# A streaming-encoder block: the embedding's loads and splits in a new order, and the gate's product and residual by whole rows

## The chip, the cores and the metric

The kernel runs on one core of one Trainium2 chip. The metric is device time in microseconds (us) of one execution; lower is better. The inputs and the output are float32 in DRAM; most matrix products are made from two fp32r parts of each operand, a high part and the remainder ("hi" and "lo"), with three matmuls (hi·hi, hi·lo, lo·hi).

## The reference, cut to what matters

```python
h = _layer_norm(x, ln_in_g, ln_in_b)
proj = h @ w_in[i]
...
mix = jnp.concatenate([o_gdn, o_fox], axis=-1) @ w_out[i]
h = _layer_norm(ALPHA * h + mix, ln1_g[i], ln1_b[i])
ff = jnp.square(jax.nn.relu(h @ w_up[i])) @ w_down[i]
ple = (p[i] @ w_ple[i]) * jax.nn.sigmoid(h @ w_ple_gate[i] + b_ple_gate[i])
h = _layer_norm(ALPHA * h + ff + ple, ln2_g[i], ln2_b[i])
```

There are 1024 tokens of width 1024; the embedding p has 256 columns, the expansion 4096.

## The kernel before, in words

The program is one long straight line of instructions. A tile scheduler orders them on each engine by program order, by priorities and by its own idea of when data are there; each engine then works through its queue strictly in that order, and semaphores hold an instruction until its inputs are there. SP issues nearly all DMAs, also in order. ACT and DVE share the splitting of operands: ACT casts the high part, DVE subtracts it from the source for the low part.

**The start.** SP loads the embedding p in two halves (`p_raw`, L227 and L239), w_ple in two halves of 512 columns (`w_raw_ple`, L233 in `load_ple`), rows of x (`load_x`), and the columns of w_in for the values in eight pieces (`wvr`, `load_wv`, L249). `load_ple` also casts and subtracts at once (L234, L54). `ple_prep(half)` transposes half of p on PE (`ps_pT`, L266), casts it on ACT (`pT_hi`, L268) and subtracts on DVE (`pT_lo`, L269). `ple_mm(t, n)` makes one block of p @ w_ple, 128 tokens by 512 columns, in six matmuls (`ps_ple`, L278), scales it by 0.5 on ACT (`ple_o`, L279) and stores it to `ple_spill` (L280). The matmuls rotate through three PSUM banks. Then come the LayerNorm of x, its transposes (`ps_tr`, L156) and the value projection (`psv`, L309), and from there the projections, the two attention groups and the output mix.

**The gate.** h @ w_ple_gate is a Strassen-like scheme of seven products for each of two halves of 256 columns (`prod`, `ps_gP`, L1075). `vals` and `plus` collect the products with the bias in a tile `gv` of 512 rows by 256 columns. `gout` takes tanh on ACT; then for each half of the rows it loads the embedding `pl` and the residual `hb`, makes (gv + 1)·pl and hb·ALPHA + gv on DVE (both at L51, the helper `stt`) and stores to `acc_spill`. It is called eight times. The same stage prepares tokens 4 to 7's blocks with `rest(j)`: three loads (`r`, L1122 to L1124, the last from `t_spill`), two DVE subtractions, transposes.

**The expansion.** `mlp_up(c)`, sixteen times, makes seven products of 12 matmuls (`ps_uP`, L1208), with operand splits `uA` and `uS` on ACT and DVE through a ring of five tiles, and the sums and activations on DVE. The last stage multiplies by w_down and adds `acc_spill`, which `with_acc` loads (L1350).

What sets the order around the change: SP's, ACT's and DVE's queues as the scheduler fills them; `tc.issue_after(x)` makes the scheduler place a step behind x; `tc.high_priority` and `tc.cur_priority` shift steps. `slot(...)` names the pool tile that a step reuses: `ph` and `pl` hold one tile of 512 KB each, `cv` and `th` three of 256 KB each.

Of the kernel before, what the change touches and what calls it, by code (L numbers as in the profile page):

```python
# [8 lines left out]
F32 = mybir.dt.float32  # L9
# [17 lines left out]
ALPHA = 2.0 ** 0.25  # L27
# [5 lines left out]
def _sl(i, n=P):  # L33
    return slice(i * n, (i + 1) * n)
# [3 lines left out]
def tile_block(ctx: ExitStack, tc: tile.TileContext, x, p, ln_in_g, ln_in_b, w_in, conv_w, a_log, dt_bias,  # L38
               gdn_norm_g, b_f, fox_norm_g, w_out, ln1_g, ln1_b, w_up, w_down, w_ple, w_ple_gate,
               b_ple_gate, ln2_g, ln2_b, out):  # L40
    nc = tc.nc
    PS = bass.MemoryType.PSUM
    x, p, out = x[0], p[0, 0], out[0]
# [6 lines left out]
    def stt(o, a, s, b, op0, op1):  # L50
        nc.vector.scalar_tensor_tensor(out=o, in0=a, scalar=s, in1=b, op0=op0, op1=op1)  # L51

    def split_lo(eng, lo, src, hi):
        eng.tensor_tensor(out=lo, in0=src, in1=hi.bitcast(F32), op=ALU.subtract)  # L54
# [157 lines left out]
    with tc.tile_pool(name="start", bufs=2, reuse_waits="tile") as stp:  # L212
# [16 lines left out]
        def load_ple(n):  # L229

            w = [wpool.tile([P, 2, 512], dt, tag=tag, name=f"{tag}_ple{n}")
                 for tag, dt in (("w_raw", F32), ("w_hi", F32R), ("w_lo", F32R))]
            nc.sync.dma_start(out=w[0], in_=w_ple[:, _sl(n, 512)].rearrange("(k q) c -> q k c", q=P))  # L233
            nc.scalar.copy(out=w[1], in_=w[0])  # L234
            split_lo(nc.vector, w[2], w[0], w[1])
            return w[1:]

        wpl = [load_ple(0)]
        nc.sync.dma_start(out=pt[:, 4:8], in_=pv[:, 4:8])  # L239
        load_x(0)  # L240
        wpl.append(load_ple(1))
        nc.gpsimd.dma_start(out=gb, in_=ln_in_g.partition_broadcast(P))
        nc.gpsimd.dma_start(out=bb, in_=ln_in_b.partition_broadcast(P))
        wvs = stp.tile([P, NK, 8], F32, name="wv_s", bufs=1)
# [17 lines left out]
        def ple_prep(half):  # L262
            for k in range(2):
                ps = sm("ps_pT")
                for i in range(4):
                    nc.tensor.transpose(ps[:, _sl(i)], pt[:, half * 4 + i, _sl(k)], ident)  # L266
                hi = pth[:, k, _sl(half, 512)]
                nc.scalar.copy(out=hi, in_=ps)  # L268
                lo = nc.vector.tensor_tensor(out=ptl[:, k, _sl(half, 512)], in0=ps, in1=hi.bitcast(F32), op=ALU.subtract)  # L269
            return lo.ins  # L270

        def ple_mm(t, n):
            so = stp.tile([P, 512], F32, tag="po", name="ple_o", bufs=5)
            ps = pj("ps_ple")
            wh, wl = wpl[n]
            for k in range(2):
                for wi, (aa, w) in enumerate(((pth, wh), (pth, wl), (ptl, wh))):
                    nc.tensor.matmul(ps, aa[:, k, _sl(t)], w[:, k], start=(k == 0 and wi == 0), stop=(k == 1 and wi == 2))  # L278
            nc.scalar.mul(out=so, in_=ps, mul=0.5)  # L279
            nc.sync.dma_start(out=ple_rows[t, :, _sl(n, 512)], in_=so)  # L280

        prep0 = ple_prep(0)
        with tc.issue_after(prep0):
            nc.vector.tensor_copy(out=wv_hi[:, :, 520:528], in_=wvs)
            split_lo(nc.vector, wv_lo[:, :, 520:528], wvs, wv_hi[:, :, 520:528])
        for t in range(4):
            ple_mm(t, 0)
        ple_prep(1)
        for t in range(4):
            ple_mm(t, 1)  # L290
# [5 lines left out]
        for t in range(NT):  # L296
# [8 lines left out]
            for n in range(2):  # L305
                ps = pj(f"psv{t}")
# [796 lines left out]

    def gout(v, n, h, t0):

        cs = slice(n * 512 + h * 256, n * 512 + h * 256 + 256)
        nc.scalar.activation(out=v, in_=v, func=AF.Tanh, scale=0.5)
        for jj in range(2):
            rows = slice(t0 * 512 + jj * 256, t0 * 512 + jj * 256 + 256)
            pl, hb = (cp.tile([P, 2, 256], F32, tag=tag, name=name, bufs=3) for tag, name in (("cv", "pl"), ("th", "hb")))  # L1110
            nc.sync.dma_start(out=pl, in_=ple_spill[rows, cs].rearrange("(j q) c -> q j c", q=P))
            nc.sync.dma_start(out=hb, in_=h1_spill[rows, cs].rearrange("(j q) c -> q j c", q=P))
            vj = v[:, 2 * jj:2 * jj + 2]
            stt(vj, vj, 1.0, pl, ALU.add, ALU.mult)
            stt(vj, hb, ALPHA, vj, ALU.mult, ALU.add)
            nc.sync.dma_start(out=acc_spill[rows, cs].rearrange("(j q) c -> q j c", q=P), in_=vj)

    def rest(j):

# [69 lines left out]
    def mlp_up(c):  # L1189
        raw = uraw.pop(c)  # L1190
        a = {f"A{f + 1}{k + 1}": raw[f][:, 4 * k:4 * k + 4] for f in range(2) for k in range(2)}
        s31, s24 = slot("kl1", [P, 2, 4, P], "wS31"), slot("va", [P, 2, 4, P], "wS24")
        a.update({"S3": s31[:, 0], "S1": s31[:, 1], "S2": s24[:, 0], "S4": s24[:, 1]})
        ua, ub = (slot(key, [P, 2, 512], name) for key, name in (("hi", "ua"), ("lo", "ub")))
        da, db = (slot("va", [P, 2, 512], name) for name in ("da", "db"))
        ps = {}

        def prod(p, chain=None):
            s, t = PAIR[p]
            v = slot(HL[hl[0] % 5], [P, 2, 4, P], f"u{s}", F32R)  # L1200
            hl[0] += 1
            hi, lo = v[:, 0], v[:, 1]
            nc.scalar.copy(out=hi, in_=a[s])  # L1203
            split_lo(nc.vector, lo, a[s], hi)
            ps[p] = ps[chain] if chain else (pj if p == "P2" else sm)(f"ps_u{p}")
            for k in range(4):
                for wi, (w, b) in enumerate(((hi, 0), (hi, 1), (lo, 0))):
                    nc.tensor.matmul(ps[p], w[:, k], B[t][b][k], start=(chain is None and k == 0 and wi == 0),  # L1208
                                     stop=(k == 3 and wi == 2), skip_group_check=chain is not None)
            return ps[p]  # L1210

        def keep(v, p):
# [24 lines left out]
        for nm in ("A11", "A12", "A22", "S3", "S1", "S2", "S4"):
            nc.sync.dma_start(out=r_spill[nm, c // 4][c % 4], in_=d[nm])
# [234 lines left out]
```

## Time and profile before

| | |
|---|---|
| runs | 1410.28, 1412.11, 1414.26 us (median 1412.11) |
| the profiled execution | 1411.87 us, span 1410.1 us |
| PE busy | 1375.8 us, 98% of the span, 7342 matmuls |
| PE weight loads busy | 1165.8 us, 83% |
| DVE busy | 1084.5 us, 77% |
| ACT busy | 559.3 us, 40% |
| DMA | 232.74 MB, mean 165 GB/s |
| mean granted clock of PE | 0.996 |

An engine is busy while it executes; a matmul's end is modelled, and matmuls overlap, so a row's duration is longer than the distance to the next. A wait is put down to the semaphore that came last. "Issue" of a DMA is when SP's instruction starts, "landing" when its semaphore rises.

### The profile page before, as it was taken

The page shows a single profiled execution, that of the slowest core. Times are in us where ns is not written, and L with a number is a line of the kernel's source. Part 1 is how long each engine was busy: PE and PEld are TensorE (multiplying, and loading weights), DVE is VectorE, ACT ScalarE, POOL GpSimd, SP SyncE. Part 2 cuts the span into 40 slices and gives each one's busy share as a digit, 9 for nine tenths or more (in the row PEclk, how much of TensorE's full clock was granted, in tenths as well). Part 3 has the DMA queues.
Part 4 walks back from the last instruction along what each step waited for, and adds up shares of the span by engine and source line. Part 5 has one row for each costly group of instructions (what it writes and reads, how often), then busy time and mean ns, then how long its engine had stood idle before and what let it go on. Part 6 is the DMA issues. An engine that isn't in the chain of part 4 may idle for free.

```text
span 1410.1 us, 20582 instructions
## 1 busy us (share of the span) xinstructions
PE 1375.8 (98%) x7342; PEld 1165.8 (83%) x7342; DVE 1084.5 (77%) x2273; ACT 559.3 (40%) x1044; POOL 15.4 (1%) x32
## 2 busy tenths in 40 slices
PE   7999999999999999999989999999999999999997
PEld 5997888988898887777889888888888888888885
DVE  6968899578566888968988766777666898748867
ACT  5323443243226767721133333333333444555421
POOL 1000000000000000000000000000000000000000
PEclk9999999999999999999999999999999999999999
DMA  9825434445478765234666744444446893334342
GB/s 304 282 104 180 150 83 116 146 157 149 127 190 199 172 150 166 68 133 168 214 215 207 237 137 153 157 160 147 148 131 228 315 342 111 97 97 125 117 134 83
DMA packets 193470, 232.74 MB, mean 165 GB/s; under 512 B 41638, under 2 KB 121687, under 8 KB 193367
## 3 DMA queue, kind: packets, MB, share of 16 engines
q1 hardware_dynamic: 187750, 226.69, 51.4%
q10 hardware_dynamic: 5232, 3.67, 1.0%
q8 instruction: 58, 0.95, 0.3%
q0 software_dynamic: 384, 1.06, 0.2%
q14 instruction: 46, 0.37, 0.1%
HBM read 155.29 MB, written 76.09 MB: 164 GB/s over the span
## 4 chain that ended last, share of the span: by engine, by line
PE 51%; DVE 3%; DMA 3%; issue 1%; SPq 0%; ACT 0%; DVEq 0%; ACTq 0%
PE ps_uP L1208 22%; PE ps_db L1328 9%; PE ps_da L1328 9%; PE ps_gP L1075 4%; PE ps_mix L954 3%; PE ps_db L1433 3%; DMA r<-t_spill 1%; DVE h L51 1%; PE ps_tr L961 1%; DMA h<-h_spill 0%; DMA wo_raw<-in_w_out_dram 0%; DMA hb<-h_spill 0%; DMA gA<-in_w_ple_gate_dram 0%; DMA h_spill<-h 0%; DVE gv L51 0%
## 5 line engine op out<-in xcount | busy, mean ns | idle before, releaser
L1208 PE MATMUL ps_uP<-T,uS 128*128 128x512 f32 x576 | 133.5, 390 | 0.0
L1208 PEld LDWEIGHTS ps_uP<-T,uS 128*128 128x128 f32 x576 | 108.1, 188 | 23.0
L1298 ACT CAST rh<-rr 128x512 fp32r<-128x512 f32 x112 | 69.9, 624 | 138.4 <-PE ps_db L1328 49.4
L54 DVE TENSOR_TENSOR rl<-rr,rh 128x512 fp32r<-128x512 f32 x112 | 77.1, 689 | 61.2 <-ACT rh L1298 22.3
L1208 PE MATMUL ps_uP<-B,uA 128*128 128x512 f32 x384 | 92.4, 396 | 0.0
L1208 PEld LDWEIGHTS ps_uP<-B,uA 128*128 128x128 f32 x384 | 72.2, 188 | 17.4
L954 PE MATMUL ps_mix<-wo,act_hi 128*128 128x512 f32 x256 | 81.7, 396 | 0.3 <-ACT act_hi L834 0.3
L207 PE MATMUL g<-act_hi,in_hi 128*128 128x512 f32 x192 | 75.5, 393 | 0.0
L207 PE MATMUL g<-act_hi,in_lo 128*128 128x512 f32 x192 | 75.3, 392 | 0.0
L207 PE MATMUL g<-act_lo,in_hi 128*128 128x512 f32 x192 | 74.9, 390 | 0.0
L54 DVE TENSOR_TENSOR uA<-uraw,uA 128x512 fp32r<-128x512 f32 x48 | 33.2, 691 | 47.8 <-ACT uA L1203 47.8
L1298 ACT CAST rl<-B 128x512 fp32r<-128x512 f32 x96 | 59.7, 623 | 24.5 <-PE ps_db L1328 11.5
L1203 ACT CAST uS<-wS 128x512 fp32r<-128x512 f32 x64 | 39.5, 624 | 73.0 <-issue 48.2
L54 DVE TENSOR_TENSOR ql<-B,rl 128x512 fp32r<-128x512 f32 x96 | 65.8, 686 | 0.3
L54 DVE TENSOR_TENSOR ptl<-ps_pt,pth 128x512 fp32r<-128x512 f32 (+2 forms) x96 | 51.1, 552 | 6.7 <-ACT pth L782 6.4
L954 PEld LDWEIGHTS ps_mix<-wo,act_hi 128*128 128x128 f32 x256 | 47.3, 188 | 10.1 <-DVE wo L54 0.6
L782 ACT CAST pth<-ps_pt 128x512 fp32r<-128x512 f32 (+2 forms) x96 | 44.4, 479 | 26.1 <-PE ps_pt L780 24.9
L51 DVE SCALAR_TENSOR_TENSOR cv<-g,hcw,cv 128x511 f32<-128x511 f32 (+2 forms) x72 | 52.8, 737 | 1.7 <-ACT cv L414 1.4
L764 ACT ACTIVATE s<-s,m 128x128 f32<-128x128 f32 (+3 forms) x64 | 49.9, 780 | 8.5 <-DVE m L761 7.8
L1328 PE MATMUL ps_db<-rl,rh 128*128 128x512 f32 x192 | 51.3, 389 | 0.0
L1328 PE MATMUL ps_db<-ql,rh 128*128 128x512 f32 x192 | 51.3, 389 | 0.0
L1328 PE MATMUL ps_db<-rl 128*128 128x512 f32 x192 | 51.3, 389 | 0.0
(358 smaller groups left out, 3586.0 us busy)
## 6 DMA issues: line engine op xcount, KB each, us to landing
uraw<-in_w_up_dram SPq DMA_DIRECT2D x32, 512.0 KB, 4.6
B<-in_w_down_dram SPq DMA_DIRECT2D x32, 512.0 KB, 5.1
rr<-rS SPq DMA_DIRECT2D x64, 256.0 KB, 2.6
in_raw<-in_w_in_dram SPq DMA_DIRECT2D x24, 512.0 KB, 4.3
rr<-rA SPq DMA_DIRECT2D x48, 256.0 KB, 2.8
h_spill<-h SPq DMA_DIRECT2D x16, 512.0 KB, 3.5
rA<-ub SPq DMA_DIRECT2D x32, 256.0 KB, 2.2
rS<-da SPq DMA_DIRECT2D x32, 256.0 KB, 2.1
```

Source lines behind the costliest of these rows:

```text
L51: nc.vector.scalar_tensor_tensor(out=o, in0=a, scalar=s, in1=b, op0=op0, op1=op1)
L54: eng.tensor_tensor(out=lo, in0=src, in1=hi.bitcast(F32), op=ALU.subtract)
L207: mm = nc.tensor.matmul(ps, w[:, k, :], a[n][:, :, k], start=(k == 0 and wi == 0), stop=(k == NK - 1 and wi == 2))
L764: nc.scalar.activation(out=s[:, :W], in_=s[:, :W], func=AF.Exp, bias=m[:, i:i + 1], scale=-1.0, accum_out=pairs[h // 2][2][:, r, j:j + 1])
L782: nc.scalar.copy(out=hi, in_=pt[:, :kn])
L954: nc.tensor.matmul(ps, a[t // 4][:, t % 4, k], w, start=(k == 0 and wi == 0), stop=(k == NK - 1 and wi == 2))
L1075: nc.tensor.matmul(ps[j // 2][:, j % 2], B[b][s][k][:, _sl(j)], a[w][:, k], start=(first and j % 2 == 0 and k == 0 and wi == 0), stop=(j % ...
L1203: nc.scalar.copy(out=hi, in_=a[s])
L1208: nc.tensor.matmul(ps[p], w[:, k], B[t][b][k], start=(chain is None and k == 0 and wi == 0), stop=(k == 3 and wi == 2), skip_group_check=c ...
L1298: nc.scalar.copy(out=hi, in_=src)
L1328: nc.tensor.matmul(ps[j], rs[x][:, _sl(j)], qs[y], start=(not chain and c == 0 and wi == 0), stop=(c == NP - 1 and wi == 2), skip_group_ch ...
L1433: nc.tensor.matmul(b[j], rs[x][:, i, _sl(j - js[0])], Q[c0 + i][y], start=(c0 == 0 and i == 0 and wi == 0), stop=(c0 + i == NP - 1 and wi ...
```

## The change

Two edits that don't touch each other.

The start: `load_ple` only loads. Both halves of w_ple are loaded directly behind the first half of p, ahead of its second half. The cast and subtraction are a step of their own, `split_ple(n)`; the first is placed behind the cast of the first half of p (`hi0`), the second behind the third scaled output block (`o[2]`).

The gate: `gout` ends with the tanh and one store of the tile, 512 KB. The product with the embedding and the residual move into `gated(t)`, which takes whole rows: for each block of 128 tokens it reads `acc_spill`, `h1_spill` and the two halves of `ple_spill`, makes the same two DVE operations for each half, and stores the rows back to `acc_spill`. It is called behind `mlp_up(c)` for c = 0 to 7. The 32 DVE operations are the same in number and size (128x512); 16 loads of `pl`, 16 of `hb` and 16 stores of 256 KB leave the gate, and 8 stores of 512 KB take their place; the expansion gets 16 loads of 512 KB, 16 of 256 KB and 8 stores of 512 KB.

```diff
             nc.sync.dma_start(out=w[0], in_=w_ple[:, _sl(n, 512)].rearrange("(k q) c -> q k c", q=P))
-            nc.scalar.copy(out=w[1], in_=w[0])
-            split_lo(nc.vector, w[2], w[0], w[1])
-            return w[1:]
-
-        wpl = [load_ple(0)]
+            return w
+
+        def split_ple(n):
+            nc.scalar.copy(out=wpl[n][1], in_=wpl[n][0])
+            split_lo(nc.vector, wpl[n][2], wpl[n][0], wpl[n][1])
+
+        wpl = [load_ple(n) for n in range(2)]
         nc.sync.dma_start(out=pt[:, 4:8], in_=pv[:, 4:8])
         load_x(0)
-        wpl.append(load_ple(1))
...
-        prep0 = ple_prep(0)
+        hi0, prep0 = ple_prep(0)
+        with tc.issue_after(hi0):
+            split_ple(0)
...
-        for t in range(4):
-            ple_mm(t, 0)
+        o = [ple_mm(t, 0) for t in range(4)]
+
+        with tc.issue_after(o[2]):
+            split_ple(1)
         ple_prep(1)
...
     def gout(v, n, h, t0):
...
         nc.scalar.activation(out=v, in_=v, func=AF.Tanh, scale=0.5)
-        for jj in range(2):
-            rows = slice(t0 * 512 + jj * 256, t0 * 512 + jj * 256 + 256)
-            pl, hb = (cp.tile([P, 2, 256], F32, tag=tag, name=name, bufs=3) for tag, name in (("cv", "pl"), ("th", "hb")))
-            nc.sync.dma_start(out=pl, in_=ple_spill[rows, cs].rearrange("(j q) c -> q j c", q=P))
-            nc.sync.dma_start(out=hb, in_=h1_spill[rows, cs].rearrange("(j q) c -> q j c", q=P))
-            vj = v[:, 2 * jj:2 * jj + 2]
-            stt(vj, vj, 1.0, pl, ALU.add, ALU.mult)
-            stt(vj, hb, ALPHA, vj, ALU.mult, ALU.add)
-            nc.sync.dma_start(out=acc_spill[rows, cs].rearrange("(j q) c -> q j c", q=P), in_=vj)
+        nc.sync.dma_start(out=acc_spill[_sl(t0, 512), n * 512 + h * 256:n * 512 + h * 256 + 256]
+                          .rearrange("(j q) c -> q j c", q=P), in_=v)
+
+    def gated(t):
+
+        v, hb = slot("ph", [P, 2, 512], "gt"), slot("pl", [P, 2, 512], "hb")
+        pl = [cp.tile([P, 512], F32, tag=tag, name="ple", bufs=3) for tag in ("cv", "th")]
+        nc.sync.dma_start(out=v.rearrange("q n c -> q (n c)"), in_=acc_spill[_sl(t), :])
+        nc.sync.dma_start(out=hb.rearrange("q n c -> q (n c)"), in_=h1_spill[_sl(t), :])
+        for n in range(2):
+            nc.sync.dma_start(out=pl[n], in_=ple_spill[_sl(t), _sl(n, 512)])
+        for n in range(2):
+            stt(v[:, n], v[:, n], 1.0, pl[n], ALU.add, ALU.mult)
+            stt(v[:, n], hb[:, n], ALPHA, v[:, n], ALU.mult, ALU.add)
+        nc.sync.dma_start(out=acc_spill[_sl(t), :], in_=v.rearrange("q n c -> q (n c)"))
...
         mlp_up(c)
+        if c < NT:
+            gated(c)
```

How the order of instructions moves, at three places.

ACT from its first cast on, before. `w_hi_ple` is the high part of half a w_ple, `pT_hi` of the transposed p, `wv_hi` of a piece `wvr` of w_in's value columns; `ple_o` is a scaled output block.

```order
L234 CAST w_hi_ple_130<-w_raw_ple_129 128x1024
L268 CAST pT_hi<-ps_pT 128x512 x2
L234 CAST w_hi_ple_139<-w_raw_ple_138 128x1024
L250 CAST wv_hi<-wvr_148 128x520
L279 ACTIVATE ple_o<-ps_ple 128x512
L250 CAST wv_hi<-wvr_152 128x520
L250 CAST wv_hi<-wvr_156 128x520
L279 ACTIVATE ple_o<-ps_ple 128x512
```

The same place on ACT in the change.

```order
L269 CAST pT_hi<-ps_pT 128x512 x2
L251 CAST wv_hi<-wvr_144 128x520
L237 CAST w_hi_ple_130<-w_raw_ple_129 128x1024
L251 CAST wv_hi<-wvr_148 128x520
L251 CAST wv_hi<-wvr_152 128x520
L251 CAST wv_hi<-wvr_156 128x520
L269 CAST pT_hi<-ps_pT 128x512 x2
L280 ACTIVATE ple_o<-ps_ple 128x512
L251 CAST wv_hi<-wvr_162 128x520
L280 ACTIVATE ple_o<-ps_ple 128x512 x2
L237 CAST w_hi_ple_134<-w_raw_ple_133 128x1024
L251 CAST wv_hi<-wvr_166 128x520
```

The first cast of w_ple went from the head of ACT's queue to behind the first piece of `wvr`; the second went from behind p's first half to behind the third output block, with three more `wvr` casts (166, 170, 174) between it and the next output block. DVE's subtractions stand in the same order: `w_lo_ple` behind `wv_lo` of the first piece, and the second behind those of 166, 170 and 174. On PE the transposes of p's second half, which stood behind the first 24 matmuls of `ps_ple`, now stand directly behind those of the first half:

```order
L267 MATMUL ps_pT<-ident,p_raw 128x128 x16
L279 MATMUL ps_ple<-w_hi_ple_130,pT_hi 128x512 x3
L279 MATMUL ps_ple<-w_lo_ple_131,pT_hi 128x512
L279 MATMUL ps_ple<-w_hi_ple_130,pT_lo 128x512
L279 MATMUL ps_ple<-w_hi_ple_130,pT_hi 128x512
```

The sixteen transposes are one run; the first three matmuls with the high part go to three banks before the first with the low part.

SP in the gate, around the loads of `rest(2)`, before: `r_7842` is the tile whose second half comes from `t_spill`, `uraw` the first columns of w_up.

```order
L1112 DMA hb<-h_spill 128x2x256
L1111 DMA pl<-ple_spill 128x2x256 x2
L1116 DMA acc_spill<-gv 128x2x256 x2
L1122 DMA r_7841<-h_spill 128x1024
L1123 DMA r_7842<-h_spill 128x512
L1124 DMA r_7842<-t_spill 128x512
L1122 DMA r_7871<-h_spill 128x1024
L1186 DMA uraw_0_8465<-in_w_up_dram 128x8x128
```

The same place in the change (here the tile is `r_7816`).

```order
L1123 DMA ple<-ple_spill 128x512 x4
L1113 DMA acc_spill<-gv 128x4x256
L1133 DMA r_7815<-h_spill 128x1024
L1134 DMA r_7816<-h_spill 128x512
L1197 DMA uraw_0_8361<-in_w_up_dram 128x8x128
L1135 DMA r_7816<-t_spill 128x512
L1133 DMA r_7845<-h_spill 128x1024
```

One store that needs only the tanh stands where two stores stood that need the DVE operations; the load of `uraw` now stands ahead of the load from `t_spill`.

DVE in the expansion, from one sum of a product to the next in c = 2 of the change. The row with `gt` and `ple` is `gated(2)`'s first operation; its other three stand a little later. Without it the rows are those of before, in nearly the same order.

```order
L48 TENSOR_TENSOR ua<-ua,ps_uP_8590 128x512
L54 TENSOR_TENSOR uS_8744<-wS_8683,uS_8744 128x512
L51 SCALAR_TENSOR_TENSOR ua<-ua 128x512
L51 SCALAR_TENSOR_TENSOR gt<-gt,ple 128x512
L48 TENSOR_TENSOR da<-ua 128x512
L48 TENSOR_TENSOR da<-ua,ub 128x512
L51 SCALAR_TENSOR_TENSOR ub<-ub 128x512
L48 TENSOR_TENSOR db<-ub,da 128x512
L48 TENSOR_TENSOR wS_8684<-uraw_1_8524,wS_8683 128x512
L48 TENSOR_TENSOR db<-ub,db 128x512
L48 TENSOR_TENSOR wS_8684<-uraw_0_8522,wS_8684 128x512
L54 TENSOR_TENSOR uS_8728<-wS_8684,uS_8728 128x512
```

One operation is added ahead of the split `uS_8728`, which the third product of the next c needs.

## Rows read from the trace of the kernel before

**Rows 1.** Windows: length, busy us of PE, PEld, DVE, ACT, POOL; PEclk, DMA share, GB/s.
```profile
5.50:37.30 31.80, 28.62 (x113) 21.86 (x114) 22.89 (x58) 17.99 (x30) 0.00 (x0) 1.00 0.96 333
37.30:690.00 652.70, 642.07 (x3801) 550.53 (x3800) 514.49 (x1295) 272.76 (x573) 11.33 (x18) 1.00 0.52 152
690.00:740.00 50.00, 44.08 (x359) 42.81 (x358) 45.52 (x71) 15.28 (x23) 0.00 (x0) 1.00 0.73 243
...
786.00:1095.00 309.00, 309.00 (x1348) 252.74 (x1347) 220.51 (x350) 102.37 (x179) 0.00 (x0) 1.00 0.51 166
```

**Rows 2.** Timeline of PE, 0 to 60: start, us, operation; [idle before, releaser].
```profile
5.49 1.94 PE L266 MATMUL ps_pT<-ident,p_raw 128*128 128x128 f32 x8 [5.49 <-DMA p_raw<-in_p_dram]
8.90 0.80 PE L278 MATMUL ps_ple<-w_hi_ple,pT_hi 128*128 128x512 f32 x1 [1.48 <-ACT pT_hi L268]
...
14.41 0.39 PE L278 MATMUL ps_ple<-w_hi_ple,pT_lo 128*128 128x512 f32 x1
14.64 0.39 PE L278 MATMUL ps_ple<-w_hi_ple,pT_hi 128*128 128x512 f32 x1
...
17.71 0.50 PE L278 MATMUL ps_ple<-w_hi_ple,pT_hi 128*128 128x512 f32 x1 [1.51 <-ACT ple_o L279]
...
37.28 1.25 PE L156 MATMUL ps_tr<-ident,h 128*128 128x128 f32 x10
```

**Rows 3.** Timeline of ACT, 0 to 45.
```profile
8.27 1.07 ACT L268 CAST pT_hi<-ps_pT 128x512 fp32r<-128x512 f32 x2
15.41 1.05 ACT L234 CAST w_hi_ple<-w_raw_ple 128x1024 fp32r<-128x1024 f32 x1 [6.07 <-DMA w_raw_ple<-in_w_ple_dram]
16.54 0.63 ACT L250 CAST wv_hi<-wvr 128x520 fp32r<-128x520 f32 x1
```

**Rows 4.** Timeline of SP, 0 to 45: the issue of the first four pieces.
```profile
4.04 8.84 SPq L249 DMA_DIRECT2D wvr<-in_w_in_dram  x4
```

**Rows 5.** DMA issues from 1.5 to 4.3: count, KB each, median us to landing.
```profile
p_raw<-in_p_dram SPq DMA_DIRECT2D x1, 512.0 KB, 7.8
...
wvr<-in_w_in_dram SPq DMA_DIRECT2D x1, 260.0 KB, 12.5
```

**Rows 6.** Timeline of DVE, 0 to 45.
```profile
16.57 1.21 DVE L54 TENSOR_TENSOR w_lo_ple<-w_raw_ple,w_hi_ple 128x1024 fp32r<-128x1024 f32 x1
17.69 2.76 DVE L54 TENSOR_TENSOR wv_lo<-wvr,wv_hi 128x520 fp32r<-128x520 f32 x4
```

**Rows 7.** Waits of PE, 40 to 60: us in total, times, longest.
```profile
PE psv L309 <- DVE act_lo L54: 0.9, 1, 0.9
```

**Rows 8.** Groups of DVE, shapes apart, 700 to 795: busy, mean ns; idle before.
```profile
L51 DVE SCALAR_TENSOR_TENSOR gv<-hb,gv 128x512 f32<-128x512 f32 x16 | 10.8, 689 | 1.2 <-DMA hb<-h_spill 1.1
...
L51 DVE SCALAR_TENSOR_TENSOR gv<-gv,pl 128x512 f32<-128x512 f32 x16 | 10.4, 687 | 2.3 <-ACT gv L1107 2.3
```

**Rows 9.** Timeline of PE, 728 to 746: the two waits.
```profile
730.75 0.66 PE L961 MATMUL ps_tr<-ident,r 128*128 128x128 f32 x4 [0.99 <-DVE T L54]
...
737.39 1.06 PE L961 MATMUL ps_tr<-ident,r 128*128 128x128 f32 x8 [1.79 <-issue]
```

**Rows 10.** Timeline of DVE, 684 to 790: the subtractions of `rest(2)`.
```profile
736.60 1.29 DVE L48 TENSOR_TENSOR r<-r,r 128x512 f32<-128x512 f32 x2 [1.50 <-DMA r<-t_spill]
```

**Rows 11.** Timeline of SP, 728 to 738: the load that they wait for.
```profile
731.45 0.44 SPq L1124 DMA_DIRECT2D r<-t_spill  x1
```

**Rows 12.** Timeline of DVE, 786 to 830: three splits and what follows.
```profile
809.05 1.89 DVE L54 TENSOR_TENSOR uS<-wS,uS 128x512 fp32r<-128x512 f32 x3
```

**Rows 13.** Timeline of PE, 784 to 830: products three to five of c = 1.
```profile
811.04 8.35 PE L1208 MATMUL ps_uP<-T,uS 128*128 128x512 f32 x36
```

**Rows 14.** DMA issues from 600 to 690: whole rows, 512 KB.
```profile
h<-h_spill SPq DMA_DIRECT2D x8, 512.0 KB, 4.0
...
h_spill<-h SPq DMA_DIRECT2D x7, 512.0 KB, 3.0
```

**Rows 15.** Windows: one stretch at the end of the attention.
```profile
574.20:577.60 3.40, 3.25 (x15) 3.11 (x16) 2.28 (x9) 1.99 (x6) 0.00 (x0) 0.50 0.53 169
```

More of the change, by code (lines that the diff above doesn't have):

```diff
@@ L267, in ple_prep @@
                 hi = pth[:, k, _sl(half, 512)]
-                nc.scalar.copy(out=hi, in_=ps)
+                last_hi = nc.scalar.copy(out=hi, in_=ps)
                 lo = nc.vector.tensor_tensor(out=ptl[:, k, _sl(half, 512)], in0=ps, in1=hi.bitcast(F32), op=ALU.subtract)
-            return lo.ins
+            return last_hi.ins, lo.ins
         def ple_mm(t, n):
@@ L274, in ple_mm @@
             ps = pj("ps_ple")
-            wh, wl = wpl[n]
+            wh, wl = wpl[n][1:]
             for k in range(2):
@@ L278, in ple_mm @@
                     nc.tensor.matmul(ps, aa[:, k, _sl(t)], w[:, k], start=(k == 0 and wi == 0), stop=(k == 1 and wi == 2))
-            nc.scalar.mul(out=so, in_=ps, mul=0.5)
+            o = nc.scalar.mul(out=so, in_=ps, mul=0.5)
             nc.sync.dma_start(out=ple_rows[t, :, _sl(n, 512)], in_=so)
-        prep0 = ple_prep(0)
+            return o.ins
+        hi0, prep0 = ple_prep(0)
+        with tc.issue_after(hi0):
+            split_ple(0)
         with tc.issue_after(prep0):
@@ L1104, in gout @@
     def gout(v, n, h, t0):
-        cs = slice(n * 512 + h * 256, n * 512 + h * 256 + 256)
         nc.scalar.activation(out=v, in_=v, func=AF.Tanh, scale=0.5)
-        for jj in range(2):
-            rows = slice(t0 * 512 + jj * 256, t0 * 512 + jj * 256 + 256)
-            pl, hb = (cp.tile([P, 2, 256], F32, tag=tag, name=name, bufs=3) for tag, name in (("cv", "pl"), ("th", "hb")))
-            nc.sync.dma_start(out=pl, in_=ple_spill[rows, cs].rearrange("(j q) c -> q j c", q=P))
-            nc.sync.dma_start(out=hb, in_=h1_spill[rows, cs].rearrange("(j q) c -> q j c", q=P))
-            vj = v[:, 2 * jj:2 * jj + 2]
-            stt(vj, vj, 1.0, pl, ALU.add, ALU.mult)
-            stt(vj, hb, ALPHA, vj, ALU.mult, ALU.add)
-            nc.sync.dma_start(out=acc_spill[rows, cs].rearrange("(j q) c -> q j c", q=P), in_=vj)
+        nc.sync.dma_start(out=acc_spill[_sl(t0, 512), n * 512 + h * 256:n * 512 + h * 256 + 256]
[11 more added lines that the diff above has]
+        nc.sync.dma_start(out=acc_spill[_sl(t), :], in_=v.rearrange("q n c -> q (n c)"))
     def rest(j):
```

## The prediction

> **What bounds the kernel now.** I read the windows first. From 37.3 us to 690 PE is busy 642.07 of 652.70 us, in the expansion 309.00 of 309.00 [rows 1]: the matmuls, which the change neither adds nor removes, set the time, and a change can win or lose only what PE waits or runs at a slow clock. There is 3.2 us of waiting in 5.5 to 37.3, 10.6 in 37.3 to 690, and 5.9 in the gate's first 50 us [rows 1]. So three places are to be costed: the start, the gate, and the expansion, which now waits for nothing and could begin to.
>
> The timelines of the start show how it hangs together. PE transposes p's first half at 5.49 as it lands, begins p @ w_ple at 8.90 and reaches the transposes of the LayerNorm at 37.28; from 14.41 to 14.64 two matmuls of 512 columns start 0.23 us apart [rows 2]. ACT casts p at 8.27, waits 6.07 us for the second w_ple, and casts the first piece of the value weights only at 16.54 [rows 3]; that piece was issued at 4.04 [rows 4] and landed 12.5 us later, at 16.5 [rows 5]. Three banks being full, PE waited 1.51 us up to 17.71 [rows 2], because the scaled output stood behind that second w_ple cast.
>
> **The start, term by term.** The change should let w_ple's cast follow p's. The instruction order says otherwise: on ACT the first w_ple cast now stands behind the cast of that first value piece. SP still issues two halves of p, two of w_ple, a block of x and a small piece ahead of it, the same bytes as before, so I take the same landing, 16.5. ACT then needs 0.6 for that cast (0.63 in [rows 3]) and 1.05 for w_ple [rows 3], and the first matmul goes from 8.90 to about 18.15: 9.25 later. That p's second half lands later costs nothing beyond this: it landed at about 9.5 as third transfer (7.8 after an issue at about 1.7, [rows 5]), the second w_ple at 15.4 as fifth [rows 3], so as fourth about 12.4, and its eight transposes end by 14.4 (1.94 in [rows 2]).
>
> From 18.15 on I count 96 matmuls. At 0.23 that is 22.2 us. Before, those from 8.90 to 14.41 ran at the low level of 1.2 GHz, some 13 of them at 0.42 instead of 0.23 (5.51 us for 13 starts, [rows 2]); I take the same 2.6 us of loss again. New waits: behind w_ple's first cast ACT has three value casts, two of p, then the outputs. The third bank fills at about 24.9, its output is out at 25.6, and the second w_ple cast, placed behind that, ends at 26.65; PE, done with its fourth block at 26.3, waits 0.35. After two matmuls it needs the fourth block's bank, whose output stands behind three value casts (1.6 us): until 28.8, a wait of 1.7. Then it needs the second low part, which DVE makes behind three subtractions of value pieces at 0.69 (2.76 for four, [rows 6]) in 1.2 [rows 6]: until 30.15, another 1.15. Sum 3.2. PE reaches the LayerNorm's transposes at 18.15 + 22.2 + 2.6 + 3.2 = 46.15, against 37.28: **+8.9**. Bounds: +6.0 if the piece lands a microsecond early and only 0.35 + 1 of the new waits come true, +10.5 if it lands a little late and the waits are a microsecond longer.
>
> What lies behind it? DVE finishes the first LayerNorm rows by about 39 (its work until then is shifted by at most 5 us) and is no longer late when PE comes; the wait of 0.9 for a low part [rows 7] should go: **−0.9**. The other waits up to 690 hang on results that PE itself gives, and move with it: 0.
>
> **The gate.** The 32 operations that leave are 16 at 0.689 and 16 at 0.687 us [rows 8], 21.2 us of DVE, and DVE's waits for `hb` of 1.1. But PE waits there only 5.9 in all [rows 1], and for particular things. The longest is 1.79 up to 737.39 [rows 9]: the transposes wait for `rest(2)`'s subtraction at 736.60, which itself waited 1.50 for its load from `t_spill` [rows 10], issued at 731.45 [rows 11], 5.1 before. SP was late with it because two stores of the gate stood ahead, waiting for the DVE operations that go. In the change the load of `uraw` stands ahead instead; it waits for a split on DVE, which about five operations fewer bring forward by some 2 us. I take issue at 729.7, landing at 734.8, one split ahead on DVE, the subtraction at 735.6 and the transposes at 736.25: 1.1 earlier, and four matmuls more done before (0.5). The wait of 0.99 at 730.75 for a split [rows 9] shortens on the way. Of the 1.6, 0.1 may be lost at `rest(3)`: **−1.5**. Bounds: 0, if `uraw`'s DVE wait takes the stores' place in full, and −3.0, half of the stage's 5.9. The tile `gv` is now stored whole by one DMA of 512 KB; its slot is needed again only several products later.
>
> **The expansion.** DVE is busy 220.5 of 309 us [rows 1]; the 21.2 come back in the first 155 us and make it 131 of 155. Enough on average, but DVE works in order. In c one operation (0.69) stands ahead of the split for the third product. Before, the first of three splits from 809.05 was done by 809.7 and its product began at 811.04 [rows 12, 13]: 1.35 us of slack, so 0.65 stays. That operation also waits for a row load that may start only when the previous rows' store has landed, in one slot. The stage frees DVE for `gated(c−1)`'s last operation about 4.7 us behind the start of that product (eight operations at 0.6, 1.89 for three in [rows 12]); 3.0 for the store and 4.0 for the load [rows 14] give 11.8, and the operation is due at 13.1 (19.3 a round, 84 matmuls at 0.23, less the 6.2 from there to the product). It holds by 1.3. In c = 0 the chain is tanh, store, load: about 3.0 + 0.4 + 3.5 + 4.0 = 11 behind the stage's start, and the sum that frees a bank follows by 15.3, due at 16.4. **0**, with bounds 0 and +3 (c = 0 a microsecond or two late, a little in each round). SP has idle time between issues here, and the stores `rA` and `rS` queued behind the waiting load have a round to land; the loads of `uraw` are a round ahead. If that cover is gone the price is the second rival. The extra 8.4 MB of traffic is 54 GB/s on the 166 of this stage [rows 1].
>
> **The sum.** 1411.87 + 8.9 − 0.9 − 1.5 + 0 = 1418.4 us. This stands against the profiled execution, 0.2 below the median of the runs; a difference of about 0.3%, 4.2 us, is what can be told from none.
>
> A rule that speaks against the change: the Trainium skill's page "TensorE: Matmul & The Clock Gate", section "Loop structure matters more than you think", says that long waits between matmuls drop the clock. By that the broken stretch at 26 to 30 us would run on at the low level; the time is the rival "clock" below. The row at 574.20 agrees that it can, and other waits here of the same length show that it need not.
>
> **The rivals.**
> - *The first piece is not waited for* (the queue gives it early, or ACT is not held). Then p's second half sets the start: first matmul at 14.4, +5.5, less the 1.7 of waits that go. With −0.9 and −1.5: 1413.3. Against it: same bytes ahead, and 12.5 us in [rows 5]. For it: "DMA: Bandwidth & Descriptors" of the Trainium skill, section "Queues, rings and completion order", says that completion is not in order of issue; no run here shows it. 15%.
> - *A loop through the store and the load in the expansion.* If store and load take 4.3 and 5.3, the chain is 4.7 + 9.6 = 14.3 against 13.1, the split passes its 0.65, and once it does the operations that follow the split come later too: a round becomes about 21 instead of 19.3. From a sum of the two of about 9 it decides; six rounds cost some 10: 1428. 7%.
> - *Clock.* After two waits near 572 the clock fell to 0.50 for 3.4 us [rows 15]. The waits of 0.35, 1.7 and 1.15 could do that once: +1.7, 1420.1. Against: no such fall after 17.71. 13%.
> - *Other side, faster: the late start is made up.* PE waits 10.6 and 5.9 later on [rows 1]. If DVE and the DMAs, 9 us ahead, lose none of that lead, all 16.5 could go: 8.9 − 16.5, 1404.2. It is faster by more than 0.3% if over 13.1 of the 16.5 go. Against: those waits hang on PE's own products. 4%.
>
> **How the numbers follow.** Forecast 61%, the rivals 15, 7, 13 and 4. The range 1412.5 to 1424 takes in the first and third rival and the sums of the bounds (+6.0 − 0.9 − 3.0 = +2.1; +10.5 + 1.7 = +12.2) and leaves out the loop and the fast case. Slower than 1416.1 needs 4.2 of the 6.5 to hold: the forecast but for a sixth of it, the clock, the loop: 0.72. Within 0.3%: the first rival and that sixth, 0.24. Faster: 0.04.
>
> **What would show it.** Right: the first `ps_ple` matmul at about 18, ACT idle from 8 to 16.5 before a cast of `wvr`, PE at the LayerNorm's transposes at about 46; the wait of 1.79 in the gate cut to under 1; PE 100% in the expansion. Wrong: a first `ps_ple` matmul before 15; idle PE before `uS` products between 800 and 950; waits between 46 and 690 that add up to under 5.

## The result and the profile after

The changed kernel takes 1427.83 us (median of 4 runs, 1424.01 to 1428.92), the kernel before on the same chip 1411.34: a ratio of 1.0106, 95% interval 1.0088 to 1.0124. It is slower by 15 us by that ratio and by 16.5 by the medians, where 6.5 were forecast, and lies above the range. The profiled execution took 1428.92 us with a span of 1427.2, 17.1 more than before.

PE runs the same 7342 matmuls in both, so the starts of matching matmuls, taken from the two traces, show where the span grew:

| stretch of PE | before | after | grew by | forecast |
|---|---|---|---|---|
| to the LayerNorm's transposes | 37.28 | 47.83 | +10.55 | +8.9 |
| from there to the gate's first product | 654.24 | 654.72 | +0.48 | -0.9 |
| gate | 94.51 | 95.40 | +0.89 | -1.5 |
| expansion | 308.55 | 313.26 | +4.71 | 0 |
| the rest, to the end of the span | | | +0.47 | 0 |

The windows of the kernel after, for the stretches of [rows 1] and with the same columns:

```profile
5.50:47.83 42.33, 30.78 (x112) 23.66 (x113) 26.33 (x69) 18.03 (x30) 0.00 (x0) 0.96 0.83 285
47.83:702.55 654.72, 644.76 (x3807) 551.61 (x3806) 512.64 (x1283) 272.38 (x573) 11.30 (x18) 1.00 0.51 150
702.55:797.95 95.40, 90.28 (x736) 88.90 (x735) 69.00 (x103) 31.73 (x44) 0.00 (x0) 0.98 0.48 158
798.07:955.00 156.93, 154.64 (x665) 123.84 (x664) 121.61 (x196) 49.33 (x86) 0.00 (x0) 1.00 0.75 246
955.00:1111.33 156.33, 156.33 (x683) 127.80 (x682) 112.98 (x180) 52.95 (x94) 0.00 (x0) 1.00 0.52 172
```

The expansion was to stay at 100%, as in [rows 1]. Its first half doesn't: PE is busy 154.64 of 156.93 us there, and DMA moves 246 GB/s against 166 over the whole stage before. The second half, without row operations, is full.

**The start** went as the order of ACT's instructions said. Timeline of ACT, and then of PE, at the start of the kernel after (compare [rows 2, 3]):

```profile
7.45 0.59 ACT L269 CAST pT_hi<-ps_pT 128x512 fp32r<-128x512 f32 x1 [0.27 <-PE ps_pT L267]
16.69 0.62 ACT L251 CAST wv_hi<-wvr 128x520 fp32r<-128x520 f32 x1 [8.66 <-DMA wvr<-in_w_in_dram]
17.22 1.04 ACT L237 CAST w_hi_ple<-w_raw_ple 128x1024 fp32r<-128x1024 f32 x1
```

```profile
18.32 1.65 PE L279 MATMUL ps_ple<-w_hi_ple,pT_hi 128*128 128x512 f32 x3 [2.96 <-ACT w_hi_ple L237]
...
20.19 0.63 PE L279 MATMUL ps_ple<-w_hi_ple,pT_lo 128*128 128x512 f32 x1
20.61 0.63 PE L279 MATMUL ps_ple<-w_hi_ple,pT_hi 128*128 128x512 f32 x1
...
26.61 0.72 PE L279 MATMUL ps_ple<-w_hi_ple,pT_hi 128*128 128x512 f32 x2 [0.22 <-ACT w_hi_ple L237]
28.68 0.50 PE L279 MATMUL ps_ple<-w_hi_ple,pT_hi 128*128 128x512 f32 x1 [1.35 <-ACT ple_o L280]
30.22 0.80 PE L279 MATMUL ps_ple<-w_lo_ple,pT_hi 128*128 128x512 f32 x1 [1.04 <-DVE w_lo_ple L54]
...
47.83 1.25 PE L156 MATMUL ps_tr<-ident,h 128*128 128x128 f32 x10
...
67.20 0.39 PE L315 MATMUL psv<-wv_hi,act_lo 128*128 128x264 f32 x1 [1.35 <-DVE act_lo L54]
```

ACT stands idle for 8.66 us in front of the first value piece, with w_ple's cast queued behind it. The three waits came in the forecast's order, with PE idle for 0.22, 1.35 and 1.04 us; counted from matmul start to matmul start they cost 3.3, against 3.2 in the forecast. What the sum lacked is the clock: behind these waits eight matmuls from 30.22 on took 3.43 us, where eight at 0.23 take 1.85. At the very beginning the pace was low too, as before the change: the starts at 20.19 and 20.61 are 0.42 apart instead of 0.23, although PEclk reads 1.00 there in both traces. Windows with a low grant (PEclk 0.50 to 0.51, the lower level of 1.2 GHz) in the kernel after, at the start, in the value product and in the gate:

```profile
29.98:33.40 3.42, 3.18 (x8) 2.50 (x9) 3.42 (x11) 0.60 (x1) 0.00 (x0) 0.51 0.10 31
67.50:70.90 3.40, 3.40 (x18) 3.40 (x17) 2.75 (x5) 0.00 (x0) 0.00 (x0) 0.51 0.51 167
719.52:722.94 3.42, 3.21 (x15) 3.21 (x16) 2.22 (x5) 0.62 (x2) 0.00 (x0) 0.50 0.97 329
```

**The expansion** shows a wait that the kernel before doesn't have. First DVE's group of the row operations that take `gt` and `ple` (busy, mean ns; idle before), from 702 to 960:

```profile
L51 DVE SCALAR_TENSOR_TENSOR gt<-gt,ple 128x512 f32<-128x512 f32 x16 | 10.9, 686 | 10.9 <-DMA gt<-acc_spill 10.7
```

DVE stood idle for 10.7 us in front of these, for the load of `gt`. Two rounds of the loop, by the timelines of SP, DVE (with the first row operation of the round before as well) and PE:

```profile
887.82 0.32 SPq L1127 DMA_DIRECT2D acc_spill<-gt  x1
892.20 0.32 SPq L1120 DMA_DIRECT2D gt<-acc_spill  x1
...
908.40 0.32 SPq L1127 DMA_DIRECT2D acc_spill<-gt  x1
912.51 0.32 SPq L1120 DMA_DIRECT2D gt<-acc_spill  x1
```

```profile
876.87 0.69 DVE L51 SCALAR_TENSOR_TENSOR gt<-gt,ple 128x512 f32<-128x512 f32 x1 [1.90 <-DMA gt<-acc_spill]
...
896.25 0.69 DVE L51 SCALAR_TENSOR_TENSOR gt<-gt,ple 128x512 f32<-128x512 f32 x1 [2.37 <-DMA gt<-acc_spill]
...
918.03 0.69 DVE L51 SCALAR_TENSOR_TENSOR gt<-gt,ple 128x512 f32<-128x512 f32 x1 [2.23 <-DMA gt<-acc_spill]
```

```profile
882.43 8.00 PE L1219 MATMUL ps_uP<-T,uS 128*128 128x512 f32 x34 [0.42 <-DVE uS L54]
901.86 0.73 PE L1219 MATMUL ps_uP<-T,uS 128*128 128x512 f32 x2 [0.30 <-ACT uS L1214]
903.01 8.04 PE L1219 MATMUL ps_uP<-T,uS 128*128 128x512 f32 x34 [0.42 <-DVE uS L54]
```

The store is issued at 887.82, the load of the same slot at 892.20, when the store has landed, and the first row operation starts at 896.25. Everything behind it on DVE is late, the splits for the third product among it, and PE waits twice. The third product starts at 881.28, 901.86 and 922.44: rounds of 20.58 us where 19.30 is a round before. Of the 1.28 a round the waits name 0.72 at most; the rest stands in the modelled durations of the matmuls beside them. Four rounds (c = 4 to 7) lost nearly all of it, 4.3 of 4.7. In the round ahead of them the operation waited for its load too, 1.29 us at 856.65, but there the slack of the splits covered all but 0.4.

### The profile page after: what moved, and what is told of

Its sections match the earlier page's. It is cut to its first block, busy times and chain, and to the rows that moved or that the text cites. A ratio compares the mean times of both kernels' runs of the same rounds, so it can differ in the third digit from the quotient of the medians.

```text
span 1427.2 us, 20554 instructions
## 1 busy us (share of the span) xinstructions
PE 1383.3 (97%) x7342; PEld 1168.3 (82%) x7342; DVE 1085.2 (76%) x2273; ACT 558.5 (39%) x1044; POOL 15.4 (1%) x32
## 4 chain that ended last, share of the span: by engine, by line
PE 45%; DVE 5%; DMA 5%; issue 1%; ACT 0%; SPq 0%; DVEq 0%; ACTq 0%
PE ps_uP L1219 13%; PE ps_db L1341 9%; PE ps_da L1341 9%; PE ps_mix L960 5%; PE ps_gP L1081 5%; PE ps_db L1446 3%; DMA acc_spill<-gt 2%; DMA gt<-acc_spill 2%; DVE gt L51 1%; DVE uS L54 1%; PE ps_tr L967 1%; DMA r<-t_spill 1%; DVE db L48 1%; DVE da L48 1%; DVE wS L48 0%
```

## The experiments

All ratios are to the kernel before, run beside them on the same chip.

**The start alone, and the gate's edit alone.** `e1_start` is the kernel before with the first half of the diff (to `ple_prep(1)`), `e2_gate` with the second (`gout`, `gated` and its call).

> The kernel before with the change's edit of the start alone (loads of w_ple and their splits); the gate and the expansion as before. Theory (three separate losses: start +10.55, a new wait and low clock near 66 us, then the expansion's loop): PE reaches the LayerNorm's transposes at 47.8, stands 11 to 13 later than before at the gate, which runs as before, and the expansion is 100% busy: 1411.3 + 11 = 1422 us, ratio 1.0078. Rival (the late start is what upsets the expansion too, by another phase of its loads): waits before uS products as in the change, 1427. Rival (the low clock near 66 us is chance): no fall there, 1420.

Measured: 1424.04 us, ratio 1.0075 (1.0059 to 1.0090). PE reaches the LayerNorm's transposes at 49.46 (first matmul at 18.93, the same three waits, a low clock twice as long as in the changed kernel); the expansion takes 308.54 us, all of it busy. The late start alone doesn't upset the expansion. The low clock near 66 us was not there; others came, one of 6.83 us in the gate among them, and the median agrees with 1422 all the same (the profiled execution, 1428.26, was the slowest of the six).

> The kernel before with the change's edit of gate and expansion alone; the start as before. Theory: LayerNorm's transposes at 37.28; the gate within 1 us of before (bounds -2 to +1), PE waits before uS products in four rounds, 1.3 each, 4.6 in all, with DVE idle for the load of gt: 1411.3 + 0 + 4.6 to 5.6 = 1416.5 us, ratio 1.0037. Rival (the expansion stalls only behind the late start): 1410 to 1412, no idle PE there.

Measured: 1415.92 us, ratio 1.0021 (1.0010 to 1.0032). The expansion of this kernel, window with the same columns:

```profile
789.63:1101.78 312.15, 310.20 (x1346) 252.07 (x1344) 234.72 (x375) 102.45 (x179) 0.00 (x0) 1.00 0.64 210
```

It is 3.6 us longer than before, with three late rounds instead of four, and without any late start. The loop belongs to the gate's edit. The two ratios together make 1.0096, the whole change 1.0106: within these intervals nothing is left that only the two together would cause.

**Other slots for the row operations.** `e3_swap` (on the changed kernel) and `e5_gate_swap` (on `e2_gate`):

```diff
-        v, hb = slot("ph", [P, 2, 512], "gt"), slot("pl", [P, 2, 512], "hb")
-        pl = [cp.tile([P, 512], F32, tag=tag, name="ple", bufs=3) for tag in ("cv", "th")]
+        pl, hb = slot("ph", [P, 2, 512], "ple"), slot("pl", [P, 2, 512], "hb")
+        v = [cp.tile([P, 512], F32, tag=tag, name="gt", bufs=3) for tag in ("cv", "th")]
```

> The changed kernel whole, but gated's tiles change places: the rows of acc_spill are loaded in two halves into the three-buffer slots that held the rows of ple_spill and stored from there, and those of ple_spill go into the one-buffer slot. The bytes, the DVE operations and the rounds stay; a load waits no longer for the landing of the store of the round before. Theory (loop through store and load): rounds of 19.3 again, no DVE wait for gt above 0.5, PE 100% from 790 on: 1427.8 - 4.6 = 1423.2 us. Rival (DVE's extra 2.7 us a round, or the transfers' traffic, delay the splits whatever the slots): the waits of 4.6 stay, 1427.8.

> The start of the kernel before, the gate of the change, and gated with its tiles changed places as in the run before this one. Theory: only the gate's difference is left, 1411.3 - 2 to + 1, about 1411; if the gate's 1.5 us of low clock do not come back, 1409.8. Rival (DVE or traffic): 1415.9 or more.

Measured: 1427.73 us, ratio 1.0101 (1.0084 to 1.0117), and 1417.49 us, ratio 1.0027 (1.0015 to 1.0039). Nothing was won: the theory missed, and the times are those of the rival, but not for its reason, since neither DVE's work nor the traffic held the rounds up one after the other. The expansions take 312.78 and 313.72 us. The four late rounds are gone, but in their place stands one wait in the fourth round, and the clock falls behind it. Timelines of DVE and of PE in `e3_swap`:

```profile
859.60 0.69 DVE L51 SCALAR_TENSOR_TENSOR gt<-gt,ple 128x512 f32<-128x512 f32 x1 [1.78 <-DMA acc_spill<-gt]
```

```profile
864.01 0.73 PE L1219 MATMUL ps_uP<-T,uS 128*128 128x512 f32 x2 [1.48 <-ACT uS L1214]
```

With other slots the order of DVE's instructions had changed too, and the row operations, moved ahead, wait for other transfers: here for the landing of a store, at 852.32 for the load of `ple` (1.76 us). So the slot alone is not the cause. That an operation waiting for a transfer ahead of the splits does the harm, whichever transfer it is, fits these rows but isn't shown by them, since the edit moved the operations as well. The next experiment keeps the slots and moves one operation.

**The place of one operation.** `e6_pin` (on the changed kernel) and `e7_gate_pin` (on `e2_gate`). `gated_ops` holds the four operations and the store of `gated`; `mlp_up` returns `end`, the squared sum of `u11`. Per round only the first of the four operations moves (in c = 5 the second too), from ahead of the third product's splits to the other three:

```diff
-        mlp_up(c)
+        end = mlp_up(c)
+        if c in range(1, NT + 1):
+            with tc.issue_after(end):
+                gated_ops(c - 1)
         if c < NT:
             gated(c)
```

> The changed kernel, but gated's four row operations are issued together behind the first squared sum of the next round, where three of them stood already: the first operation leaves its place ahead of the three splits of the third product. The slots, the transfers, the bytes and the DVE work stay. Theory (the place of that operation, which waits on DVE for the store and the load of its slot, is the loop): store to load to operation takes 4.4 + 5 of some 17 us that are free, rounds of 19.3, no PE wait before uS products: 1427.8 - 4.6 = 1423.2 us. Rival (traffic or DVE's load): rounds above 20 stay, 1427.8.

Measured: 1423.75 us, ratio 1.0086 (1.0074 to 1.0099). The window of the expansion, and a round of DVE:

```profile
796.42:1104.96 308.54, 308.54 (x1345) 252.32 (x1344) 235.21 (x375) 102.22 (x179) 0.00 (x0) 1.00 0.64 213
```

```profile
895.98 2.49 DVE L54 TENSOR_TENSOR uS<-wS,uS 128x512 fp32r<-128x512 f32 x4
...
900.79 1.29 DVE L51 SCALAR_TENSOR_TENSOR gt<-gt,ple 128x512 f32<-128x512 f32 x2
```

The expansion takes 308.54 us, as before the change, with DVE as busy as in the changed kernel (235.21 against 234.58 us) and the traffic no less (213 GB/s against 209). The row operations wait for nothing. This settles the expansion: the cause is neither DVE's work nor the traffic alone, but the place of the one operation whose load comes round through its own store. Where it stands now, 16.8 us lie between the store's issue and the next first operation; in the changed kernel a round of 19.3 left 8.35.

> The start of the kernel before, the gate of the change, and gated with its operations placed as in the run before this one: what the gate's edit is worth once the loop is gone. Theory: the gate comes out between -1 and +1 with the expansion at 100%: 0.999 to 1.001 of before. Rival (as forecast, the gate gives 1.5): 0.9985 or less. Rival (the expansion is slowed by the traffic): 1.002 or more, as for the gate's edit alone.

Measured: 1412.48 us, ratio 1.0002 (0.9992 to 1.0013). The expansion takes 308.55 us, the gate 93.41 against 94.51 before. The profiled execution of this kernel granted the full clock in the gate, so the gate's edit is worth 1.1 us there; over all runs it can't be told from nothing. The rival that forecast 0.9985 or less for the gate did not come.

**The start's first cast.** `e4_split0`, on the changed kernel:

```diff
         wpl = [load_ple(n) for n in range(2)]
+        split_ple(0)
...
-        with tc.issue_after(hi0):
-            split_ple(0)
```

> The changed kernel, but the first w_ple is cast and split at once, as in the kernel before, and no longer behind p's first half: on ACT it stands first again, ahead of the first cast of a value piece. The loads keep the change's order, the second w_ple its split behind the third output. Theory (the start's +10.55 is this one cast waiting behind the piece that lands at 16.5): first ps_ple matmul at 9, LayerNorm's transposes at 37.3 to 39, 1427.8 - 9 = 1418.5 us. Rival (the order of the loads, or the second split behind the outputs, costs most): transposes at 42 or later, 1422 to 1428.

Measured: 1418.55 us, ratio 1.0046 (1.0033 to 1.0058). Timeline of PE:

```profile
8.69 0.80 PE L280 MATMUL ps_ple<-w_hi_ple,pT_hi 128*128 128x512 f32 x1 [1.23 <-ACT pT_hi L270]
...
21.33 1.00 PE L280 MATMUL ps_ple<-w_hi_ple,pT_hi 128*128 128x512 f32 x3 [0.96 <-ACT w_hi_ple L237]
23.21 0.50 PE L280 MATMUL ps_ple<-w_lo_ple,pT_hi 128*128 128x512 f32 x1 [0.89 <-DVE w_lo_ple L54]
28.00 0.50 PE L280 MATMUL ps_ple<-w_hi_ple,pT_hi 128*128 128x512 f32 x1 [1.03 <-ACT ple_o L281]
40.69 1.25 PE L156 MATMUL ps_tr<-ident,h 128*128 128x128 f32 x10
```

The time is as expected, the start not quite: 40.69 instead of at most 39. That the time fits all the same is in part luck: in the profiled execution the stretch from there to the gate is 1.9 us shorter than in the changed kernel (no fall of the clock near 67) and the expansion 1.7. The first cast's place is 7.1 of the 10.55 us (47.83 to 40.69). The other 3.4 are mostly the waits of 0.96, 0.89 and 1.03: the second w_ple, split behind the third output, and an output behind value casts.

**A start with ACT's order mended.** `e8_cast` (gate and expansion as before) splits the first w_ple at once and ties the value casts behind the third output; the first LayerNorm, tied behind p's first subtraction before, is tied to a later output of ACT.

```diff
+        with tc.issue_after(o[2]):
+            split_wv(0)
+            load_wv(4)
+            split_wv(4)
...
-            with tc.issue_after(prep0) if t == 0 else ExitStack():
+            with tc.issue_after(o1[1]) if t == 0 else ExitStack():
```

Here `split_wv` holds the casts and subtractions of `load_wv`, and `o1` the outputs of the second w_ple's first four blocks.

> The gate and expansion of the kernel before. The start: both w_ple loads early as in the change, the first split at once, and the casts of the value pieces issued behind the third output, so that ACT never waits for a piece ahead of an output. Theory (ACT's order decides the start): first ps_ple matmul at 9, no PE wait of 1.5 near 17, 1.5 to 2 less than before by the end of p @ w_ple: ratio 0.9985 to 1.000. Rival (the pieces, loaded later, hold the value product up): PE waits of 2 or more near 38 to 45, ratio 1.001 or more.

Measured: 1416.19 us, ratio 1.0034 (1.0021 to 1.0047). The theory missed; the rival's ratio came, but not its wait near 38 to 45. Timeline of DVE:

```profile
14.46 0.69 DVE L130 BATCH_NORM_STATS2 st<-x 128x6 f32<-128x512 f32 x1 [4.37 <-DMA x<-in_x_dram]
15.07 0.67 DVE L276 TENSOR_TENSOR pT_lo<-ps_pT,pT_hi 128x512 fp32r<-128x512 f32 x1
```

The same error on the other engine: the tie to an output of ACT did not hold DVE's instructions, so the LayerNorm's statistics went ahead of p's second subtraction, and waited 4.37 us for x; PE waited 3.58 for that subtraction. `e9_both` ties the value casts behind the casts of p's second half (`hi1`), their low parts behind p's subtraction (`lo1`), the LayerNorm behind the first four low parts, and splits the second w_ple behind the second output; its gate and expansion are those of `e7_gate_pin`. `e10_start2` is that start with the gate and expansion of the kernel before.

```diff
+        with tc.issue_after(o[1]):
+            split_ple(1)
+        hi1, lo1 = ple_prep(1)
...
+                with tc.issue_after(hi1):
+                    nc.scalar.copy(out=wv_hi[:, k, 0:520], in_=raw)
+                with tc.issue_after(lo1):
+                    last = split_lo(nc.vector, wv_lo[:, k, 0:520], raw, wv_hi[:, k, 0:520])
```

> A start with ACT's order mended, and the gate and row operations of the run in which these stood together behind the next round's first squared sum. The start: both w_ple loads early as in the change, the first split at once, the second behind the second output, the casts of the value pieces behind those of p's second half, their low parts and the first LayerNorm behind p's. Theory (ACT's and DVE's order alone decide the start, and no load is late for PE): first ps_ple matmul at 9, no wait of 1.5 near 17, LayerNorm's transposes at 35.5 to 36.5 against 37.28, gate -1 without a fall of the clock: 1.5 to 2.5 less than before, ratio 0.998 to 0.999. Rival (the second four value pieces, whose slots come free later, or the first rows of LayerNorm, hold PE up near 36 to 45): waits there of 1.5 or more, ratio 1.000 or more.

> The mended start of the run before this one alone, with the gate and expansion of the kernel before. Theory: LayerNorm's transposes at 35.5 to 36.5, 1 to 1.7 less than before: ratio 0.9988 to 0.9993, and the difference to the run before is the gate's. Rival (value pieces or LayerNorm late): 1.000 or more.

Measured: 1411.75 us, ratio 0.9988 (0.9976 to 1.0001), and 1412.87 us, ratio 0.9993 (0.9980 to 1.0006). Both land on the expected ratio, but with 1.0 still inside the intervals. `e9_both` is the best kernel of the study, 1.2% under the changed one; that it beats the kernel before is not shown. Timeline of PE in `e9_both`:

```profile
8.77 0.79 PE L288 MATMUL ps_ple<-w_hi_ple,pT_hi 128*128 128x512 f32 x1 [1.53 <-ACT pT_hi L278]
...
35.79 1.38 PE L156 MATMUL ps_tr<-ident,h 128*128 128x128 f32 x8
38.77 0.63 PE L156 MATMUL ps_tr<-ident,h 128*128 128x128 f32 x4 [0.90 <-DVE h L51]
```

The wait of 1.51 of [rows 2] is gone and the LayerNorm is reached 1.5 earlier, but there DVE's first rows end the next wait, 0.90. The matching matmuls near 53 us start 0.0 to 0.3 later than before the change: the start's gain was given back within 20 us.

## Why the prediction was wrong

The sign and the mechanism of the largest term were right, the sum was 10.6 us too low for the profiled execution (17.1 against 6.5). Step by step:

- **"First matmul to about 18.15": right**, 18.32. That the cast behind the first value piece is the cause is shown by `e4_split0`. The three waits, forecast as 3.2, cost 3.3. "I take the same 2.6 us of loss again" was the step that failed here. The low pace at the beginning came as taken: twelve matmuls from 18.32 to 23.43, a loss of 2.3. (The 2.6 rested on a miscount: from 8.90 to 14.41 the kernel before starts 11 matmuls, not 13, a loss of 3.0.) But the clock fell once more behind the waits (the window from 29.98), and that cost another 1.6: 18.32 + 22.2 + 2.3 + 3.3 + 1.6 is 47.7. The clock rival gave this 1.7, with a chance of 13%, and the sum held no term for it. It came in all four profiled executions with this start (the changed kernel, `e1_start`, `e3_swap`, `e6_pin`).
- **"The wait of 0.9 should go": wrong.** It became 1.35, at 67.20, because DVE waited 1.89 us for a block of x at 64.13, and the clock fell behind it. Before the gate most of that came back: the fall of [rows 15] was absent, and two waits, at 317 and 660, were shorter by 1.4 and 1.2. The rest of the 654 us moved along, as argued.
- **"The gate: -1.5": right only at full clock.** Without a fall it gave 1.1 (`e7_gate_pin`: 93.41 against 94.51). There the step "I take issue at 729.7" came nearly true: the load from `t_spill` was issued 38.4 behind the gate's start, 1.5 earlier than in [rows 11], and the wait of 1.79 [rows 9] was 0.99. Timelines of SP and of PE in `e7_gate_pin`:

```profile
729.27 0.57 SPq L1135 DMA_DIRECT2D r<-t_spill  x1
```

```profile
735.75 1.06 PE L961 MATMUL ps_tr<-ident,r 128*128 128x128 f32 x8 [0.99 <-issue]
```

  In the changed kernel a fall, at 719.52, turned the gain into +0.89. The load was issued no earlier than before (742.55, the gate having started 11.03 later), and its wait stayed at 1.65. The forecast's upper bound, 0, was to come from `uraw`'s wait for DVE; but `uraw` waited only 0.2. SP stood 3.8 us, up to 739.97, in front of the first of the three loads, until PE's transposes had read the rows that the tile held. That load was issued 37.4 behind the gate's start here and 37.3 in `e2_gate`, both with a fall, and 36.0 and 35.9 in `e7_gate_pin` and `e6_pin`, without one. Waits of SP from 736 to 740.2 (in total, times, longest), then timelines of SP and PE, all of the changed kernel:

```profile
SPq L1133 <- PE ps_tr L967: 3.8, 1, 3.8
```

```profile
739.97 0.32 SPq L1133 DMA_DIRECT2D r<-h_spill  x1
...
742.08 0.43 SPq L1197 DMA_DIRECT2D uraw<-in_w_up_dram  x1
742.55 0.74 SPq L1135 DMA_DIRECT2D r<-t_spill  x1
```

```profile
716.66 0.39 PE L1081 MATMUL ps_gP<-gA12h,B 128*128 128x256 f32 x1 [1.14 <-ACT gA12h L1091]
719.73 0.58 PE L1081 MATMUL ps_gP<-gA12l,B 128*128 128x256 f32 x1 [1.81 <-DVE gA12l L54]
...
749.51 1.06 PE L967 MATMUL ps_tr<-ident,r 128*128 128x128 f32 x8 [1.65 <-issue]
```

  The fall does not belong to the change's gate: with the gate of the kernel before, `e10_start2` had one as well (96.0 us for the gate, a fall at 710.00) and `e1_start` a longer one (97.8), where `e8_cast` had none (95.0). That the profiled execution of the kernel before had none in its 94.51 is, as far as these traces show, chance.

- **"It holds by 1.3": the step that cost most.** The chain was the right one, and so was the room for it: of a round of 19.3 the stretch from the first row operation to the store takes 10.95 (876.87 to 887.82 in the rows above; the same in five of six rounds), which leaves 8.35 for store and load. The mis-sized terms are these two: "3.0 for the store and 4.0 for the load", 7.0 together, were 8.4 to 9.6 in the late rounds, from the store's issue to the operation. In c = 4 and 5 it was the store (5.3 and 4.4 up to the load's issue, then 4.0 and 4.1 for the load), in c = 6 and 7 the load (5.5 and 5.8, after 4.1 and 3.5). The 3.0 and 4.0 are medians of [rows 14], from a stretch where DMA's share was 0.44 (600 to 690) and single stores took 2.6 to 6.0 us; in the expansion's first half, which the change itself loads, the share is 0.75. That load was sized too low as well: the 8.4 MB are what the whole kernel moves more, while the counts under "The change" give the expansion 16.8 MB; 80 GB/s came on top in its first half (246 against 166), where 54 were forecast. How far the traffic made the transfers longer, and how far they spread anyway, no run here separates. DMA issues of the kernel after, 798 to 955 (median us to landing):

```profile
gt<-acc_spill SPq DMA_DIRECT2D x8, 512.0 KB, 3.9
hb<-h_spill SPq DMA_DIRECT2D x8, 512.0 KB, 5.4
acc_spill<-gt SPq DMA_DIRECT2D x8, 512.0 KB, 4.4
```

The late rounds took 9.3, 8.4, 9.6 and 9.3, all above 8.35. The rival named the mechanism and nearly its point ("about 9"), and its round of 21 was 20.1 to 20.6; I gave it 7%, as if the margin of 1.3 were sure, though both terms were read from a quieter stage. Its 1428 is close to the measured time only by chance: it counted 10 for the loop, and the loop cost 4.7.

So slower, at 0.72, was the right side, and the upper end of the range was too low: it was made from the start's bound and the clock alone, without the expansion's own bound of +3, and both came.

The Trainium skill's "TensorE: Matmul & The Clock Gate", section "Loop structure matters more than you think", speaks of long waits between matmuls that let the clock drop. The traces agree that falls follow waits (at 29.98, 67.50 and 719.52), but not that the same waits always bring one: in the gate `e2_gate` waited 1.13 and 1.44 us and the clock fell, `e6_pin` and `e7_gate_pin` waited 1.14 and 1.45 and it did not. Where the second wait there was longer (1.81 in the changed kernel, 1.82 in `e4_split0`, 2.40 in `e3_swap` and `e5_gate_swap`), a fall came each time. What decides at 1.45 stayed open. With the change's gate, the five profiled executions that had the fall took 95.2 to 96.4 us for it, the three that had none 93.4 to 93.8.

## What to carry to other kernels

When work is moved into a stage that is full, look at the first of its operations that waits for a transfer, and at what stands behind it on that engine: in this kernel one 0.69 us operation ahead of the splits cost 4.7 us, and the same operation a few places later cost nothing. A transfer's time for such a chain is read from a stage as busy as the one it moves to, the change's own traffic included, and a margin smaller than the spread of its landings is no margin. A split or cast "as soon as its data can be there" helps only if nothing that lands later is queued ahead of it.

## What was not expected of the hardware

Transfers of the same size landed after very different times. Single stores of 512 KB took 2.6 to 6.0 us before the change, between 600 and 690, where the DMA share was 0.44; in the expansion's first half after it, at 0.75, seven took 3.5 to 5.6 up to the issue of the load that waits for them. Of the 512 KB loads there, those of `gt` took 3.9 in the median and those of `hb`, issued beside the stores, 5.4; between 600 and 690 the median was 4.0 [rows 14]. And the granted clock fell, or not, behind waits of the same length in the same place of nearly the same program, as told above.
